# Convolution taps as ScalarE products, weight casts a unit ahead, and two more combined pairs of x in a one-core encoder block

## The chip, the cores and the metric

The kernel runs on one core of a Trainium2 chip. A core has TensorE (PE, matmuls into PSUM; PEld is its weight loads), VectorE (DVE), ScalarE (ACT), GpSimd (POOL) and SyncE (SP, which here only issues transfers). The metric is the device time in microseconds of one launch, lower is better; the time before is the median of 3 runs.

## The reference

One layer of a hybrid encoder on 256 tokens of width 4096, in float32:

```python
def reference(x, p, norm_in_g, w_in, rel_table, w_dw, b_dw, conv_ln_g, ..., final_g):
    ...
    xn = rms_norm(h, norm_in_g[i])
    proj = xn @ w_in[i]                     # 4096 x 14336
    q, k, v, z_a, a_c, g_c, z_c = jnp.split(proj, ..., axis=-1)
    y_a = chunked_attention(q, k, v, rel_table[i])   # 16 heads of 128, 4 chunks of 64
    y_a = rms_norm(y_a, attn_out_g[i]) * jax.nn.silu(z_a)
    y_c = conv_module(a_c, g_c, w_dw[i], b_dw[i], conv_ln_g[i], conv_ln_b[i], w_pw[i], b_pw[i])
    y_c = rms_norm(y_c, conv_out_g[i]) * jax.nn.silu(z_c)
    h = h + jnp.concatenate([y_a, y_c], axis=-1) @ w_out[i]
    gate = jax.nn.sigmoid(rms_norm(h, ple_norm_g[i]) @ w_ple_gate[i] + b_ple_gate[i])
    h = h + gate * (p[i] @ w_ple[i])
    return rms_norm(h, final_g)

def conv_module(a, g, w_dw, b_dw, ln_g, ln_b, w_pw, b_pw):
    u = a * jax.nn.sigmoid(g)
    ...     # causal depthwise convolution along time, 31 taps, + b_dw
    u = jax.nn.silu(layer_norm(u, ln_g, ln_b))
    return u @ w_pw + b_pw
```

## The kernel before

Activations lie transposed in SBUF: `xT` is eight `big` tiles of 4 blocks of 128 rows, each split into a high part (rounded to the matmul's float32r) and a low part. A product adds three matmuls for each 128 x 128 block of x and 512 columns of weights: high x high, low x high, high x low. So each weight tile `wt` (128 x 1024 floats, 512 KB by one transfer on SP's queue, five buffers) is split too: ScalarE casts it to `wh`, VectorE subtracts `wl = wt - wh` (lines 202 and 203 in `parts_of`, three buffers each).

There are two kinds of product. `product` takes 512 columns and runs over K in steps of two blocks (two row halves x two blocks x three = 12 matmuls a step, line 216). `mixed_product` takes two sets of 512 columns and runs over 16 *units* of two K blocks each. A plain unit has 24 matmuls (line 352). A unit marked `*` ("seven") is *combined*: by a 2 x 2 scheme with seven products instead of eight it needs 21 matmuls, and for it VectorE makes sums of weights (`ua`, `ub`, lines 399 to 404), which are split like weights; sums of x lie ready in `xS`. Its helper products P1, P5, P6, P7 take four banks of `ps_tmp`, the pool that the transposes and the attention use too; on the last combined unit `helper_sums` frees them. Which units are combined, and in which order, is a text such as `early = "1 3 5 7 0* 9 2* 11 4* 13 6* 15 8 10 12 14"`.

The order of the work: first `g_c` and `a_c` of 512 channels by `product`. Then four groups g. In each, `glu_conv(g + 1)` makes a and g of the next 512 channels by a mixed product with order `early`, gates and transposes them to `uT`, and queues their 31 x 4 taps in `later`: each one a VectorE instruction of 128 x 256 (line 594). `heads(g)` then makes q and k by another mixed product with `early`, transposes them, makes v by `product`, and runs the attention of four heads in one go. `fill(n)` after a unit takes n items from `later`: four in these mixed products, two in `product`. In the last group `layer_norm_swish` puts the layer norm in `later`, its sums on POOL. Then come the pointwise product (line 848), the gates z_a and z_c (`gated`, orders `delayed` and `dense`), the output product (`late`, `dense`), and the embedding gate (`late`, `steady`), the last two blocks of columns by `product`.

Apart from a few pinned instructions at the start, the order on each engine is laid out ahead of the run by a planner that takes the earliest instruction of the program that it expects to be ready. Each engine then runs its list in order.

Of the kernel before, what the change touches and what calls it, by code (L numbers as in the profile page):

```python
# [19 lines left out]
FIRST = 2  # L20
WARM = (5, 3, 2)
# [5 lines left out]
def hybrid_block(  # L27
# [31 lines left out]
    PAD = TAPS - 1  # L59
# [14 lines left out]
    wpool = pool("wpool", 5)  # L74
# [8 lines left out]
    upool = pool("upool", 2, first_sums)  # L83
    more = None

# [3 lines left out]
    pin = tc.keep_in_program_order  # L89


    gin_rows = spool.tile([KD, P], F32, tag="s", name="gin_rows")
# [3 lines left out]
    w_in0 = w_in[0]  # L96
# [11 lines left out]
    idle = spool.tile([P, NB], mybir.dt.bfloat16, tag="pT", name="idle")  # L108
# [84 lines left out]

    def part_tiles():
        return [wpool.tile([P, KC, NB], F32R, tag=tag, name=tag, bufs=3) for tag in ("wh", "wl")]

    def parts_of(wt, kc, tiles=None):
        if tiles is None:
            tiles = part_tiles()
        wh, wl = tiles  # L200
        made = (
            nc.scalar.copy(wh[:, :kc, :], wt[:, :kc, :]),  # L202
            nc.vector.tensor_tensor(  # L203
                wl[:, :kc, :], wt[:, :kc, :], wh[:, :kc, :].bitcast(F32), ALU.subtract
            ),
        )
        return (wh, wl), made
# [13 lines left out]

    def product(w, col, lhs, kblocks, pool=None, tag="acc", ahead=None, lag=(), begun=None, fills=2):
# [94 lines left out]
    def pair_parts(src):  # L317

        tiles = [upool.tile([P, 2, NB], F32R, tag=tag, name=tag) for tag in ("uh", "ul")]
        return parts_of(src, 2, tiles)[0]  # L320

    def units(text):

        return [(int(u.rstrip("*")), u.endswith("*")) for u in text.split()]


    steady = units("1 0* 3 2* 5 4* 7 6* 9 8* 11 10* 13 12* 15 14")
    dense = units("1 0* 3 2* 5 4* 6* 7 8* 9 10* 11 12* 14* 13 15")
    delayed = units("1 3 5 7 0* 9 2* 11 4* 13 6* 15 8* 10 12 14")
    early = units("1 3 5 7 0* 9 2* 11 4* 13 6* 15 8 10 12 14")  # L330
    late = units("1 3 5 7 9 11 13 15 0* 2 4* 6 8* 10* 12 14")

    def mixed_product(
# [29 lines left out]
        last_seven = max(n for n, (_, seven) in enumerate(order) if seven)  # L363
        for n, (pair, seven) in enumerate(order):
            if ahead:
                ahead(pair)
            wts = []
            for k in range(2):
                wt = wpool.tile([P, 2, NB], F32, tag="w", name="wt")
                kb = 2 * pair + k  # L370
                rows = w[kb * P : (kb + 1) * P, :]
                nc.sync.dma_start(
                    wt,
                    bass.AP(
                        tensor=rows.tensor, offset=rows.offset + col,
                        ap=[list(rows.ap[0]), [apart, 2], [1, NB]],
                    ),
                )
                wts.append(wt)
            if not seven:  # L380
                for k in range(2):
# [12 lines left out]
            w0, w1 = wts  # L394
            ua = upool.tile([P, 2, NB], F32, tag="u", name="ua")
# [665 lines left out]
```

## Time and profile before

| | us |
|---|---|
| median of 3 runs (2059.16 to 2062.18) | 2061.59 |
| span of the profiled execution (its time is given as this span) | 2059.9 |
| PE busy | 2031.9 (99%) |
| PEld busy | 1671.2 (81%) |
| DVE busy | 1823.0 (88%) |
| ACT busy | 1151.5 (56%) |
| POOL busy | 42.9 (2%) |

The profile is of one execution. "Busy" is the time in which an engine had an instruction running; recorded durations of neighbours overlap, so the spacing of starts is the better price. Ends of matmuls are modelled. Transfers moved 412.27 MB, 200 GB/s on average, with the 16 transfer engines' queue at 62.5%.

### The profile page before, as it was taken

The numbers are of one execution on the slowest core, as the hardware profiler recorded it, in microseconds if no ns is written. First come the engines' busy times: TensorE is split into PE (matmuls) and PEld (weight loads), VectorE is DVE, ScalarE is ACT, GpSimd is POOL, SyncE is SP. The second block draws the span as 40 slices with busy tenths as digits, with TensorE's granted clock in tenths as the row PEclk, the third lists the DMA queues.
The fourth block names the chain that finished last, engine by engine and source line by source line (L and its number), as shares of the span: only waits on it lengthen the run. The fifth ranks groups of instructions, "written<-read, shape, count | busy, mean of one in ns | idle before, by whom it ended". The sixth has DMA issues, their size and how long they took to land.

```text
span 2059.9 us, 25890 instructions
## 1 busy us (share of the span) xinstructions
PE 2031.9 (99%) x9145; PEld 1671.2 (81%) x9145; DVE 1823.0 (88%) x2543; ACT 1151.5 (56%) x1477; POOL 42.9 (2%) x37
## 2 busy tenths in 40 slices
PE   9999999999999999999999999999999999999997
PEld 6888888887888787788888888878888888888886
DVE  7599999999977998875889999899999999999954
ACT  7455535554564535575556656576565666656543
POOL 0000000000000002300000000000000000000010
PEclk9999999999999999999999999999999999999999
DMA  8666666656566665655666666676666656666664
GB/s 286 189 181 204 189 200 183 198 185 191 177 205 185 194 189 163 187 186 194 192 209 200 200 217 196 215 232 205 213 202 205 213 184 201 203 228 210 219 209 165
DMA packets 170331, 412.27 MB, mean 200 GB/s; under 512 B 13006, under 2 KB 16222, under 8 KB 170202
## 3 DMA queue, kind: packets, MB, share of 16 engines
q1 hardware_dynamic: 169914, 410.11, 62.5%
q8 instruction: 71, 1.16, 0.2%
q10 hardware_dynamic: 288, 0.52, 0.1%
q14 instruction: 58, 0.48, 0.1%
HBM read 406.39 MB, written 4.19 MB: 199 GB/s over the span
## 4 chain that ended last, share of the span: by engine, by line
PE 89%; DVE 6%; DMA 2%; issue 2%; ACT 1%; POOL 0%; SPq 0%; ACTq 0%; POOLq 0%; DVEq 0%
PE acc L352 53%; PE acc L216 21%; PE acc_P L352 13%; DVE wl L203 2%; DMA wt<-in_w_in_dram 1%; DVE cv L594 1%; DMA xin<-in_x_dram 1%; PE tmp_ps L161 1%; DVE ul L203 1%; PE tmp_ps L744 0%; PE tmp_ps L759 0%; PE tmp_ps L777 0%; ACT wh L202 0%; DVE ub L403 0%; PE tmp_ps L619 0%
## 5 line engine op out<-in xcount | busy, mean ns | idle before, releaser
L202 ACT CAST wh<-wt 128x1024 fp32r<-128x1024 f32 x739 | 726.0, 991 | 626.4 <-PE acc L352 314.0
L352 PE MATMUL acc<-wh,big_t 128*128 128x512 f32 x3344 | 1038.4, 391 | 3.6 <-ACT big_t L147 2.9
L203 DVE TENSOR_TENSOR wl<-wt,wh 128x1024 fp32r<-128x1024 f32 x739 | 849.7, 1161 | 130.0 <-ACT wh L202 124.4
L352 PEld LDWEIGHTS acc<-wh,big_t 128*128 128x128 f32 x3344 | 626.4, 188 | 133.1 <-ACT big_t L147 3.4
L352 PE MATMUL acc<-wl,big_t 128*128 128x512 f32 x1672 | 652.1, 391 | 3.4 <-DVE wl L203 3.3
L216 PE MATMUL acc<-wh,big_t 128*128 128x512 f32 x1248 | 389.2, 392 | 3.2 <-DVE big_t L148 1.3
L352 PEld LDWEIGHTS acc<-wl,big_t 128*128 128x128 f32 x1672 | 314.0, 188 | 72.0 <-DVE wl L203 7.3
L216 PEld LDWEIGHTS acc<-wh,big_t 128*128 128x128 f32 x1248 | 233.3, 188 | 52.7 <-DVE big_t L148 2.2
L216 PE MATMUL acc<-wl,big_t 128*128 128x512 f32 x624 | 243.1, 390 | 0.1
L594 DVE SCALAR_TENSOR_TENSOR cv<-uT,dw,cv 128x256 f32<-128x256 f32 x480 | 214.4, 487 | 1.0
L202 ACT CAST uh<-ub 128x1024 fp32r<-128x1024 f32 x103 | 108.4, 1052 | 113.2 <-DVE ub L404 92.1
L352 PE MATMUL acc_P<-uh,big_t 128*128 128x512 f32 x534 | 163.7, 390 | 0.0
L202 ACT CAST uh<-ua 128x1024 fp32r<-128x1024 f32 x103 | 108.5, 1054 | 62.4 <-DVE ua L400 57.9
L216 PEld LDWEIGHTS acc<-wl,big_t 128*128 128x128 f32 x624 | 117.1, 188 | 24.4 <-DVE wl L203 0.5
L203 DVE TENSOR_TENSOR ul<-ub,uh 128x1024 fp32r<-128x1024 f32 x103 | 128.2, 1245 | 8.1 <-ACT uh L202 7.6
L203 DVE TENSOR_TENSOR ul<-ua,uh 128x1024 fp32r<-128x1024 f32 x103 | 125.9, 1222 | 0.3
L352 PEld LDWEIGHTS acc_P<-uh,big_t 128*128 128x128 f32 x534 | 100.0, 188 | 21.2 <-ACT uh L202 0.5
L352 PE MATMUL acc_P<-ul,big_t 128*128 128x512 f32 x267 | 103.7, 393 | 0.9 <-DVE ul L203 0.8
L399 DVE TENSOR_TENSOR ua<-wt 128x512 f32<-128x512 f32 x103 | 71.6, 695 | 31.7 <-DMA wt<-in_w_in_dram 21.4
L400 DVE TENSOR_TENSOR ua<-wt 128x512 f32<-128x512 f32 x103 | 70.9, 689 | 3.7 <-DMA wt<-in_w_in_dram 3.0
L404 DVE TENSOR_TENSOR ub<-ub,wt 128x512 f32<-128x512 f32 x103 | 72.2, 701 | 1.2
L403 DVE TENSOR_TENSOR ub<-ua,wt 128x512 f32<-128x512 f32 x103 | 71.0, 689 | 0.2
(201 smaller groups left out, 1350.8 us busy)
## 6 DMA issues: line engine op xcount, KB each, us to landing
wt<-in_w_in_dram SPq DMA_DIRECT2D x447, 512.0 KB, 4.1
wt<-in_w_out_dram SPq DMA_DIRECT2D x128, 512.0 KB, 4.2
wt<-in_w_ple_gate_dram SPq DMA_DIRECT2D x128, 512.0 KB, 4.1
wt<-in_w_pw_dram SPq DMA_DIRECT2D x32, 512.0 KB, 4.4
hc<-in_x_dram SPq DMA_DIRECT2D x8, 512.0 KB, 5.0
wt<-in_w_ple_dram SPq DMA_DIRECT2D x8, 512.0 KB, 4.5
out_dram<-hc SPq DMA_DIRECT2D x16, 256.0 KB, 2.9
xin<-in_x_dram SPq DMA_DIRECT2D x7, 512.0 KB, 8.9
```

Of the source, the lines that this page charges most:

```text
L161: nc.tensor.transpose(pt[:, i * T + h * P : i * T + (h + 1) * P], src[:, h, b * P : (b + 1) * P], ident,)
L202: nc.scalar.copy(wh[:, :kc, :], wt[:, :kc, :]),
L203: nc.vector.tensor_tensor(wl[:, :kc, :], wt[:, :kc, :], wh[:, :kc, :].bitcast(F32), ALU.subtract),
L216: nc.tensor.matmul(acc, a, b[:, k, :], start=kb == 0 and kind == 0, stop=kb == kblocks - 1 and kind == 2,)
L352: nc.tensor.matmul(banks[name], a, b, start=name not in begun, stop=final and ends[name] == n and kind == 2,)
L399: plus(ua[:, 0], w0[:, 0], w0[:, 1])
L400: plus(ua[:, 1], w0[:, 1], w1[:, 1])
L403: plus(ub[:, 0], ua[:, 0], w1[:, 1])
L404: plus(ub[:, 1], ub[:, 0], w1[:, 0])
L594: nc.vector.scalar_tensor_tensor(cv[:, i, :], uT[:, i, k : k + T], dw[:, b, k : k + 1], cv[:, i, :], ALU.mult, ALU.add,)
```

## The change

- Each tap becomes four ScalarE activations (`tap_products`: u times the tap's column, into a tile `prod`) and one VectorE sum of 128 x 1024 (`tap_sum`), instead of four VectorE multiply-adds. The tile is shifted by the tap's offset, so `uT` needs no zeros in front.
- `plan` lists every unit in order; `prepare` issues the transfers and ScalarE casts of the next unit in the midst of the one before, and `take` hands them out. `chain` fixes the order of casts, subtractions, weight sums and taps on ScalarE and on VectorE as the program has it.
- `early` has six combined units instead of four, so `xS` has three tiles, made of six blocks of x.
- The ends of a group (scaling of the accumulators, gate, transposes, scores, values, squares) are put in `closing`, and each `fill` takes one step of it. Taps go by weight: one for a product, three for a sum; plain units of the groups' mixed products give four, combined ones none, steps of the value product four.
- Combined units add weights in place in `wt`; `wh` and `wl` have five buffers; first and last units of a product go bank by bank; PSUM copies of qT, kT and pT move to ScalarE, the layer norm's sums from POOL to VectorE.

```diff
+AG = (4,0)
+QK = (4,0)
+VF=4
+WB = 5
+HB = 5
...
-    upool = pool("upool", 2, first_sums)
+    upool = pool("upool", 3, first_sums)
     more = None
+    more_scratch = []
...
+    def chain(ins):
+
+        prev = last_of.get(ins.ins.engine)
+        if prev is not None:
+            tc.add_manual_dep(
+                ins.ins, prev.name,
+                mybir.DependencyInfo(mybir.DependencyClass.NoSync, mybir.DependencyReason.DATA),
+                reason="order of the parts",
+            )
+        last_of[ins.ins.engine] = ins.ins
+        return ins
...
+    closing = deque()
+
+    def step():
+        if closing:
+            closing.popleft()()
+
+    def finish_steps():
+        while closing:
+            step()
 
     def fill(n):
-        for _ in range(min(n, len(later))):
-            later.popleft()()
+        step()
+        credit[0] += n
+        while later and credit[0] > 0:
+            item = later.popleft()
+            weight, item = item if isinstance(item, tuple) else (1, item)
+            credit[0] -= weight
+            item()
+        if not later:
+            credit[0] = 0
...
     def part_tiles():
-        return [wpool.tile([P, KC, NB], F32R, tag=tag, name=tag, bufs=3) for tag in ("wh", "wl")]
+        return [wpool.tile([P, KC, NB], F32R, tag=tag, name=tag, bufs=HB) for tag in ("wh", "wl")]
 
     def parts_of(wt, kc, tiles=None):
         if tiles is None:
             tiles = part_tiles()
         wh, wl = tiles
         made = (
-            nc.scalar.copy(wh[:, :kc, :], wt[:, :kc, :]),
-            nc.vector.tensor_tensor(
+            chain(nc.scalar.copy(wh[:, :kc, :], wt[:, :kc, :])),
+            chain(nc.vector.tensor_tensor(
                 wl[:, :kc, :], wt[:, :kc, :], wh[:, :kc, :].bitcast(F32), ALU.subtract
-            ),
+            )),
         )
         return (wh, wl), made
...
+    early = units("1 3 5 0* 7 9 2* 11 4* 13 6* 15 8* 12 10* 14")
...
+    def prepare():
+
+        if prepared or not plan:
+            return
+        unit = plan.popleft()
+        w, col, apart, at, kind = unit
+        wts, highs = [], []
+        if kind == "one":
+            wt = wpool.tile([P, KC, NB], F32, tag="w", name="wt")
+            nc.sync.dma_start(
+                wt,
+                w[at * P : (at + KC) * P, col : col + NB].rearrange("(k q) n -> q k n", q=P),
+            )
+            wts.append(wt)
+        else:
+            for k in range(2):
+                wt = wpool.tile([P, 2, NB], F32, tag="w", name="wt")
+                kb = 2 * at + k
+                rows = w[kb * P : (kb + 1) * P, :]
+                nc.sync.dma_start(
+                    wt,
+                    bass.AP(
+                        tensor=rows.tensor, offset=rows.offset + col,
+                        ap=[list(rows.ap[0]), [apart, 2], [1, NB]],
+                    ),
+                )
+                wts.append(wt)
+        for k, wt in enumerate(wts):
+            n = 1 if kind == "seven" and k == 0 else 2
+            highs.append(part("wh"))
+            chain(nc.scalar.copy(highs[k][:, :n], wt[:, :n]))
+        prepared.append((unit, wts, highs))
+
+    def take(*unit):
+
+        prepare()
+        found, wts, highs = prepared.pop()
+        assert found[1:] == unit[1:] and found[0] is unit[0], (found, unit)
+        return wts, highs
...
-            wh, wl = weight_parts(w, col, k0, kc, lag[kept.index(k0)] if keep else None)
+            if lag:
+                wh, wl = weight_parts(w, col, k0, kc, lag[kept.index(k0)] if keep else None)
+            else:
+                (wt,), (wh,) = take(w, col, None, k0, "one")
+                wl = part("wl")
+                minus(wl, wt, wh)
+                prepare()
...
-    early = units("1 3 5 7 0* 9 2* 11 4* 13 6* 15 8 10 12 14")
...
-            wts = []
...
+            (w0, w1), (h0, h1) = take(w, col, apart, pair, "seven" if seven else "pair")
+            l0, l1 = part("wl"), part("wl")
             if not seven:
-                for k in range(2):
-                    wh, wl = parts_of(wts[k], 2)[0]
-                    for j in range(2):
-                        for h in range(NH):
-                            name = (("P2", "P3"), ("P4", "X"))[h][j]
-                            add(name, block(2 * pair + k, h), (wh[:, j], wl[:, j]), n, k == 1)
-                fill(fills)
+                for wt, wh, wl in ((w0, h0, l0), (w1, h1, l1)):
+                    minus(wl, wt, wh)
+                prepare()
+                fill(fills[0] if isinstance(fills, tuple) else fills)
+                parts = ((h0, l0), (h1, l1))
+                places = [(k, j, h) for k in range(2) for j in range(2) for h in range(NH)]
+                if n in (0, len(order) - 1):
+                    places = [(k, j, h) for j in range(2) for h in range(NH) for k in range(2)]
+                for k, j, h in places:
+                    name = (("P2", "P3"), ("P4", "X"))[h][j]
+                    add(name, block(2 * pair + k, h), [t[:, j] for t in parts[k]], n, k == 1)
                 continue
             begins = not helper
             if begins:
                 for name in ("P1", "P5", "P7", "P6"):
                     helper[name] = ps_tmp.tile([P, NB], F32, tag="tmp", name=f"acc_{name}")
                 banks.update(helper)
-            w0, w1 = wts
-            ua = upool.tile([P, 2, NB], F32, tag="u", name="ua")
-            ub = upool.tile([P, 2, NB], F32, tag="u", name="ub")
-            plus = partial(nc.vector.tensor_tensor, op=ALU.add)
-            w0h, w0l = parts_of(w0, 1)[0]
-            plus(ua[:, 0], w0[:, 0], w0[:, 1])
-            plus(ua[:, 1], w0[:, 1], w1[:, 1])
-            uah, ual = pair_parts(ua)
-            w1h, w1l = parts_of(w1, 2)[0]
-            plus(ub[:, 0], ua[:, 0], w1[:, 1])
-            plus(ub[:, 1], ub[:, 0], w1[:, 0])
-            ubh, ubl = pair_parts(ub)
+            minus(l0[:, :1], w0[:, :1], h0[:, :1])
+            plus(w0[:, 0], w0[:, 0], w0[:, 1])
+            minus(l1, w1, h1)
+            plus(w0[:, 1], w0[:, 1], w1[:, 1])
+            ah, bh = part("wh"), part("wh")
+            chain(nc.scalar.copy(ah, w0))
+            plus(w1[:, 1], w0[:, 0], w1[:, 1])
+            plus(w1[:, 0], w1[:, 1], w1[:, 0])
+            chain(nc.scalar.copy(bh, w1))
+            prepare()
+            fill(fills[1] if isinstance(fills, tuple) else fills)
+            al, bl = part("wl"), part("wl")
+            minus(al, w0, ah)
+            minus(bl, w1, bh)
...
+            add("P1", block(k0, 0), (h0[:, 0], l0[:, 0]), n, True)
+            add("P2", block(k1, 0), (h1[:, 0], l1[:, 0]), n, True)
+            add("P3", s_of(3), (h1[:, 1], l1[:, 1]), n, True)
+            add("P5", s_of(1), (ah[:, 0], al[:, 0]), n, True)
+            add("P7", s_of(0), (ah[:, 1], al[:, 1]), n, True)
+            add("P6", s_of(2), (bh[:, 1], bl[:, 1]), n, True)
+            add("P4", block(k1, 1), (bh[:, 0], bl[:, 0]), n, True)
...
-        for h, j in QUARTERS:
-            stt(
-                z[h][j], c[h][j], r[:, h : h + 1], z[h][j],
-                ALU.mult, ALU.subtract if j else ALU.add,
-            )
+
+        def finals():
+            for h, j in QUARTERS:
+                stt(
+                    z[h][j], c[h][j], r[:, h : h + 1], z[h][j],
+                    ALU.mult, ALU.subtract if j else ALU.add,
+                )
+
+        closing.append(finals)
...
+    def tap_products(made, uT, c, n):
+        dst = act.tile([P, 4, T], F32, tag="act", name="prod" if n else "cv")
+        made.append(dst)
+        for i in range(4):
+            b = 4 * c + i
+            chain(nc.scalar.activation(
+                dst[:, i, : T - n], uT[:, i, : T - n], AF.Identity,
+                scale=dw[:, b, TAPS - 1 - n : TAPS - n], bias=0.0 if n else bdw[:, b : b + 1],
+            ))
+
+    def tap_sum(made, n):
+        cv = made[0]
+        chain(nc.vector.tensor_tensor(cv[:, :, n:], cv[:, :, n:], made[n][:, :, : T - n], ALU.add))
...
+            sg, gate = scaled_pair(w_in0, o_a + c * NB, o_g - o_a, AG_ORDER, r_x, AG)
+
+            def gate_u():
+                for h in range(NH):
+                    nc.scalar.activation(gate[:, h, :], gate[:, h, :], AF.Sigmoid)
+                    tt(sg[:, h, :], sg[:, h, :], gate[:, h, :], ALU.mult)
+
+            closing.append(gate_u)
...
+        def begin_taps():
+            turn(1)
+            later.append((1, lambda: (tap_products(made, uT[0], c, 0), conv.append(made[0]))))
+            for n in range(1, TAPS):
+                later.append((1, lambda n=n: tap_products(made, uT[0], c, n)))
+                if n > 1:
+                    later.append((3, partial(tap_sum, made, n - 1)))
+            later.append((3, partial(tap_sum, made, TAPS - 1)))
+
+        closing.append(partial(turn, 0))
+        closing.append(begin_taps)
+        if c == 0:
+            finish_steps()
...
-        add = nc.gpsimd.tensor_tensor
+        add = nc.vector.tensor_tensor
...
+        closing.append(lambda: (turn(qT, q), load_bias()))
+        closing.append(lambda: turn(kT, k))
+        for hd in range(GH):
+            closing.append(partial(scores, hd))
+            if hd:
+                closing.append(partial(turn_p, hd - 1))
+        closing.append(partial(turn_p, GH - 1))
         if g == n_g - 1:
             first_sums.close()
             more = pool("more", 4)
-        accv = product(w_in0, o_v + g * NB, xT, KD)
-        v = spool.tile([P, NH, NB], F32, tag="hd", name="v", bufs=5)
-        for h in range(NH):
-            nc.scalar.activation(v[:, h, :], accv[h], AF.Identity, scale=r_x[:, h : h + 1])
-        attention(g, qT, kT, v, bias)
-
-    n_g = H // GH
+            second()
+        accv = product(w_in0, o_v + g * NB, xT, KD, fills=VF)
+        finish_steps()
+        closing.append(evacuate_v)
+        for hd in range(0, GH, 2):
+            closing.append(lambda hd=hd: (values(hd), values(hd + 1)))
+        closing.append(squares)
+
     assert n_g == CW // NB
-    xS = [big_tile(upool) for _ in range(2)]
-    for c in range(4):
+    xS = [big_tile(upool) for _ in range(3)]
+    for c in range(6):
...
```

More of the change, by code (lines that the diff above doesn't have):

```diff
@@ L106, in hybrid_block @@
         )
-    idle = spool.tile([P, NB], mybir.dt.bfloat16, tag="pT", name="idle")
+    idle = spool.tile([P, NB], mybir.dt.bfloat16, tag="s", name="idle", bufs=2)
     nc.vector.memset(idle, 0.0)
@@ L222, in product, with plus @@
+    def plus(out, a, b):
+        return chain(nc.vector.tensor_tensor(out, a, b, ALU.add))
     def product(w, col, lhs, kblocks, pool=None, tag="acc", ahead=None, lag=(), begun=None, fills=2):
@@ L1015, in hybrid_block @@
         if c < n_f - 1:
[L1016 removed]
+            acc = product(w_ple_gate0, c * NB, hT, KD)
             for h in range(NH):
```

277 lines of the change are left out of this document (145 added, 132 removed).

## The prediction

> **What bounds the kernel now.** I read the page first: busy shares, then the chain that ended last.
>
> ```profile
> span 2059.9 us, 25890 instructions
> PE 2031.9 (99%) x9145; PEld 1671.2 (81%) x9145; DVE 1823.0 (88%) x2543; ACT 1151.5 (56%) x1477; POOL 42.9 (2%) x37
> PE 89%; DVE 6%; DMA 2%; issue 2%; ACT 1%; POOL 0%; SPq 0%; ACTq 0%; POOLq 0%; DVEq 0%
> ```
>
> TensorE is busy 99% and holds 89% of the chain, VectorE 6%. Ends of matmuls are modelled, so the real rate is read from an unbroken run of the chain in order of time (start, length, what).
>
> ```profile
> 62.54 43.54 PE acc L216 x192
> 420.15 17.50 PE acc L352 x77
> ```
>
> 43.54/192 and 17.50/77 both give 0.227 us for one 512-column matmul. The kernel issues 8,619 such product matmuls (counted from the code): 8,619 x 0.227 = 1,955 us of the 2,059.9. What is left, some 105 us, is transposes and attention on TensorE, the start, the tail and waits. So two things can move the time: fewer matmuls, or fewer waits. The waits, by stage: TensorE and its weight loads between 107 us (convolution and attention groups begin) and 1,010 us (pointwise product ends), then the weight loads from 1,010 to 1,340 us.
>
> ```profile
> PE acc L352 <- DVE wl L203: 3.3, 4, 1.6
> PE tmp_ps L744 <- DVE z L462: 1.7, 2, 1.3
> PE acc_P L352 <- DVE ul L203: 0.8, 2, 0.5
> PEld acc L352 <- DVE wl L203: 7.3, 12, 2.0
> PEld tmp_ps L782 <- DVE pT L779: 3.1, 14, 0.6
> PEld tmp_ps L777 <- ACT s L770: 2.9, 10, 0.4
> PEld acc_P L352 <- DVE ul L203: 2.8, 6, 0.9
> PEld tmp_ps L744 <- DVE z L462: 2.7, 4, 1.8
> PEld acc L352 <- DVE z L874: 0.7, 1, 0.7
> ```
>
> Nearly all waits for VectorE are in the groups: 5.8 us seen on matmuls, 18.8 us on weight loads, of which part is covered by the matmul still running. I take 13 us of real loss, near the middle. The last row is the whole of 1,010 to 1,340 us: there is nothing to win in the gates, only something to lose. The stages:
>
> ```profile
> 0.00:38.00 38.00, 33.39 (x150) 23.86 (x151) 24.82 (x45) 27.65 (x61) 1.15 (x10) 1.00 0.89 312
> 38.00:107.40 69.40, 69.40 (x325) 57.50 (x325) 42.87 (x58) 35.97 (x47) 1.02 (x2) 1.00 0.64 192
> 323.70:548.00 224.30, 222.63 (x1013) 183.53 (x1012) 215.81 (x348) 114.52 (x143) 0.51 (x2) 1.00 0.62 190
> 1010.00:1340.00 330.00, 329.70 (x1456) 272.76 (x1455) 306.61 (x370) 195.63 (x217) 3.01 (x1) 1.00 0.64 205
> 1433.00:1680.00 247.00, 247.00 (x1096) 204.53 (x1095) 235.69 (x276) 147.68 (x175) 0.00 (x0) 1.00 0.62 206
> ```
>
> (stretch, length, then busy PE, PEld, DVE, ACT, POOL, granted clock, DMA share, GB/s). The clock is 1.00 throughout. One whole group, 323.7 to 548 us, has VectorE at 215.8 of 224.3 us and ScalarE at 114.5: VectorE is the engine that makes TensorE wait, ScalarE has room.
>
> **The change part by part.** Prices are spacings of neighbouring starts, since recorded durations overlap.
>
> ```profile
> 125.29 0.70 DVE L403 TENSOR_TENSOR ub<-ua,wt 128x512 f32<-128x512 f32 x1
> 125.89 0.49 DVE L594 SCALAR_TENSOR_TENSOR cv<-uT,dw,cv 128x256 f32<-128x256 f32 x1
> 126.29 0.70 DVE L404 TENSOR_TENSOR ub<-ub,wt 128x512 f32<-128x512 f32 x1
> 127.68 1.24 DVE L203 TENSOR_TENSOR wl<-wt,wh 128x1024 fp32r<-128x1024 f32 x1
> 128.82 1.24 DVE L203 TENSOR_TENSOR ul<-ub,uh 128x1024 fp32r<-128x1024 f32 x1
> ```
>
> So VectorE pays 0.60 for 512 columns, 0.40 for a tap, 1.14 for 1,024 columns.
>
> *Six combined pairs.* `early` goes from four to six combined units in 3 + 4 = 7 mixed products: 14 more combined units, each 21 matmuls instead of 24. 14 x 3 x 0.227 = **-9.5 us** of TensorE, which is on the path everywhere. Each costs VectorE 5 x 0.60 + 3 x 1.14 = 6.4 us against 2 x 1.14 = 2.3 for a plain one, so +8.2 us for two in a product. The third combined x tile adds two `combine_again`, about 5 us at these prices, to VectorE in 38 to 107 us, where 26 us are free (second stretch above): nothing.
>
> *Taps.* Per group VectorE loses 124 taps x 0.40 = 49.6 us and gets 30 wide sums x 1.14 = 34.2; the copies of qT, kT (4 x 0.60) and pT (4 x about 0.5) also go to ScalarE. Net for a group: 16.4 - 49.6 + 34.2 - 4.4 = -3.4 us, while TensorE's need falls 2.7. VectorE therefore stays near full; what changes is where its work lies. At before's four taps a unit a mixed product needed 12 x 2.3 + 4 x 6.4 + 64 x 0.40 + ends = 79 us plus some 5 for scalings and helper sums, against 84 us of matmuls. Afterwards it is 10 x 2.3 + 6 x 6.4 + about 8 x 1.14 + 5 = 76 against 83, and the value product takes 16 x 1.14 + 16 x 1.14 + 7 = 43 against 43.5 plus some 5 us of small TensorE work. That is cover, barely.
>
> ScalarE's price for a tap product (128x226 to 256, SBUF, one column as scale) is not in the trace. Its bounds:
>
> ```profile
> 890.59 1.63 ACT L712 CAST big_t<-cv 128x256 fp32r<-128x256 f32 x5
> 877.90 2.57 ACT L702 ACTIVATE cv<-cv,prm 128x256 f32<-128x256 f32 x5
> 1342.49 1.54 ACT L147 ACTIVATE big_t<-tmp_ps,prm 128x256 fp32r<-128x256 f32 x4
> 858.03 1.98 ACT L202 CAST wh<-wt 128x1024 fp32r<-128x1024 f32 x2
> ```
>
> Taking off a last instruction of 0.41, 0.59, 0.47 and 1.05 us, the spacings are 0.31 (no column operand), 0.50 (two), 0.36 (one, from PSUM) and 0.93. Nearest is one column: 0.39, between the ends. 496 x 0.39 = 193 us more ScalarE (ends 154 and 248), in all about 1,380 of 2,050. On average it lies beside TensorE; the tight place is a value product: 16 casts x 0.93 + 16 taps x 4 x 0.39 + exponentials, copies and table load about 9 = 49 us beside some 48.5. The casts run ahead there by up to four of the five `wh` tiles, so I cost it at nothing; at 0.50 it is 56 us, 7 too many, three times.
>
> The Trainium skill, "ScalarE: Activation LUTs", Rules for kernel authors, says the opposite of this edit: multiply and add belong on VectorE, not ScalarE. Its section What ACT_TABLE_LOAD costs gives 186 ns + 0.833 ns an element, 93 ns for each pointer operand, 93 ns of overlap back to back; my estimate from these figures at 241 columns is 0.387 us a tap, and the sum would be the same 2047. By the rule taken as a bound, the third rival below is the outcome; the 56% busy of ScalarE speaks against it.
>
> *Fixed order, casts a unit ahead.* No instruction is added; `chain` adds order, not waits. But a cast that waits for its weights now holds ScalarE's taps and PSUM copies behind it, and those hold TensorE's transposes. The combined unit also works in place in `wt`, so both weight tiles stay taken to the unit's end, with five as before; SP's queue already stands at that point:
>
> ```profile
> SPq L372 <- DVE wl L203: 939.8, 430, 6.7
> wt<-in_w_in_dram SPq DMA_DIRECT2D x447, 512.0 KB, 4.1
> ```
>
> The second tile of the next combined unit starts when the first tile of this one is freed: 4.1 us to land, 0.93 cast, 5.1 in all. VectorE covers it with its last subtraction 1.14, the plain unit 2.3 and the next unit's first two steps 1.2 = 4.6 plus a fill. So 0 to 0.5 us may be missing per combined unit. The gate and output stretches above leave VectorE 23.4 + 11.3 us idle over 29 + 24 combined units, 0.65 each: covered on average, not in every place. I take +2 us (ends 0 and 15).
>
> *Group ends spread out.* Scalings, transposes, scores and values come one step a unit, and first and last units fill and free banks one by one. This aims at the 13 us: L744, L777, L782 and the L203 waits where taps met the ends. Ends: 0 (they only move) and -13. I take -8, the larger part, since the arithmetic above gives VectorE 7 us of slack in a mixed product. The bias table is loaded later, two value units (5.4 us) ahead of its use, on SP's queue with its waits: I leave part of the 13 standing for it. The layer norm's sums move from POOL to VectorE, 6 x 1.14 + 2 x 0.9 = 9 us in the last group, where the convolution is over: no cost.
>
> *Start.* Each x chunk now stands behind one more 512 KB weight transfer on SP. At 312 GB/s that is 1.7 us; the stretch to 38 us has DMA at 0.89. Ends 0 and +1.7; I take +1.
>
> Sum: 2059.9 - 9.5 - 8 + 2 + 1 = 2045.4; the median of the runs is 1.7 above the profiled span, so **2047 us**. Not touched: gates, output and embedding products in count, and the tail.
>
> **Rivals.** *All waits go* and nothing new comes: 2061.6 - 9.5 - 13 = 2039. For it: all those waits name work the change moves. Against: VectorE still at 96% in the groups. *The waits only move*: 2061.6 - 9.5 + 3 = 2055, or with a few us more at each of 18 product boundaries no change, 2060. For it: VectorE's sum falls only as much as TensorE's. *ScalarE becomes the bound* of the value products at 0.50 us a tap: 3 x 7 to 3 x 10 us, 2047 + 25 = 2072; the point is about 0.45. *Slower by weight tiles*: in place, 75 combined units after 1,010 us each lose 1.0 us of VectorE against 0.65 of slack: 75 x 0.35 = 26, so 2045 + 26 = 2071; it decides from about 0.85 us each, and speaks through SP's 939.8 us of waits for exactly these tiles. Against: the 4.6 us of cover.
>
> **How the numbers follow.** Forecast (2040 to 2053) 0.45; all waits go (under 2040) 0.12; waits only move, 2053 to 2057.5, 0.13, and 2057.5 to 2065.7, 0.10; the two slower mechanisms 0.12 (tiles) and 0.08 (ScalarE). 0.2% of 2061.6 is 4.1 us, about what a measurement here tells from no change. So faster 0.70, same 0.10, slower 0.20. The range 2036 to 2066 leaves 0.04 below and 0.16 above.
>
> **What would show it.** 8,577 product matmuls at 0.227 us; no L594 group on VectorE, but some 496 ScalarE activations near 0.48 us recorded, 0.39 apart; ScalarE busy near 1,380 us, VectorE near 1,790. In one middle group 224.3 us should become about 217. Wrong if weight loads wait for ScalarE casts in the value products, if rows `PEld acc <- DVE wl` appear after 1,010 us with more than 5 us, or if the stretch 0 to 107 us grows by more than 2.

## The result and the profile after

The changed kernel takes 2046.76 us (median of 4 runs, 2045.93 to 2047.58) against 2061.89 for the one before (4 runs, 2059.16 to 2064.21): ratio 0.9928, 95% interval 0.9914 to 0.9942. 2047 was forecast. The profiled execution took 2046.57, 1.8 above its span. From the page: span, busy shares, the chain by engine, and the two groups that make the taps now.

```profile
span 2044.8 us, 26229 instructions
PE 2018.8 (99%) x9103; PEld 1667.0 (82%) x9103; DVE 1816.4 (89%) x2241; ACT 1370.8 (67%) x2033; POOL 14.7 (1%) x23
PE 95%; ACT 1%; DVE 1%; DMA 1%; issue 1%; ACTq 0%; POOLq 0%; POOL 0%; DVEq 0%
L714 ACT ACTIVATE prod<-uT,dw 128x255 f32<-128x255 f32 (+14 forms) x480 | 201.0, 490 | 3.7 <-DVE cv L721 3.6
L721 DVE TENSOR_TENSOR cv<-cv,prod 128x1020 f32<-128x1020 f32 (+14 forms) x120 | 138.5, 1154 | 20.3 <-ACT prod L714 20.2
```

VectorE's share of the chain fell from 6% to 1%, and TensorE's rose from 89% to 95%. With the 16 first taps, which carry the bias, there are 496 activations. The stretches that answer to those shown of before, with the same columns (start; a middle group; its value product; the pointwise product; the gates z; three output products):

```profile
0.00:104.70 104.70, 100.91 (x464) 79.99 (x465) 69.61 (x112) 65.53 (x110) 1.70 (x9) 1.00 0.74 239
323.10:542.30 219.20, 219.20 (x1002) 182.08 (x1001) 202.34 (x228) 179.17 (x304) 0.30 (x1) 1.00 0.62 197
492.70:542.30 49.60, 49.60 (x238) 41.23 (x237) 45.19 (x58) 49.46 (x104) 0.30 (x1) 1.00 0.61 185
901.20:995.50 94.30, 89.72 (x387) 73.31 (x386) 60.73 (x84) 49.28 (x74) 0.69 (x1) 0.96 0.61 201
995.50:1326.10 330.60, 330.40 (x1467) 273.59 (x1465) 314.13 (x374) 195.77 (x220) 1.67 (x1) 1.00 0.61 204
1416.90:1664.50 247.60, 246.97 (x1097) 204.09 (x1095) 241.83 (x281) 148.91 (x179) 0.00 (x0) 1.00 0.62 206
```

Two stretches of before that were not shown yet, its middle value product and its pointwise product:

```profile
503.30:548.20 44.90, 44.90 (x205) 37.23 (x204) 44.49 (x77) 16.78 (x17) 0.00 (x0) 1.00 0.62 188
916.80:1010.60 93.80, 93.80 (x434) 77.19 (x433) 60.08 (x91) 48.86 (x78) 0.69 (x1) 1.00 0.59 189
```

The middle group is full of TensorE work now (219.20 of 219.20) and 5.3 us shorter than before's 224.5 between the same two matmuls. In its value product ScalarE is busy for 49.46 of 49.60 us: full, but TensorE does not stand. The waits of TensorE from 107 to 1,010 us, and the first rows of those of its weight loads:

```profile
PE acc L255 <- ACT wh L304: 4.5, 1, 4.5
PE acc L446 <- DVE wl L321: 0.4, 1, 0.4
```

```profile
PEld acc L255 <- ACT wh L304: 5.0, 1, 5.0
PEld acc L446 <- DVE wl L321: 0.8, 1, 0.8
```

Before, the rows shown for VectorE came to 5.8 us on matmuls and 15.9 on weight loads here; with the row for ScalarE (2.9) the latter are the 18.8 of the prediction. Of VectorE's waits 0.4 and 1.9 us are left; in their place stands one wait of 4.5 to 5.0 us for ScalarE that had not been there. The timeline of its place, the start of the pointwise product (start, length, instruction):

```profile
899.51 5.00 ACT L852 CAST big_t<-cv 128x256 fp32r<-128x256 f32 x16
904.41 2.16 ACT L963 ACTIVATE y_a<-tmp_ps,den 128x128 f32<-128x128 f32 x8
906.42 0.66 ACT L562 ACTIVATE junk<-y_a 128x512 bf16<-128x512 f32 x1
...
907.65 4.85 ACT L304 CAST wh<-wt 128x1024 fp32r<-128x1024 f32 x5
908.77 1.22 PE L255 MATMUL acc<-wh,big_t 128*128 128x512 f32 x2 [4.54 <-ACT wh L304]
```

At the end of the last group the program issues what is left of the side work and of the group's end in one go. One weight unit was cast ahead; the second cast stands on ScalarE behind sixteen splits, eight evictions and the squares, until 907.65. The matmuls on both sides of the pause start at 903.84 and 908.77 us, 4.7 us further apart than usual. And the pause has an aftermath. The same place by the granted clock (third number from the right):

```profile
901.20:903.80 2.60, 2.60 (x14) 2.16 (x13) 2.60 (x9) 2.60 (x10) 0.00 (x0) 1.00 0.00 0
903.80:908.80 5.00, 0.46 (x3) 0.03 (x1) 1.97 (x8) 5.00 (x17) 0.54 (x1) 0.76 0.00 0
908.80:913.00 4.20, 4.16 (x9) 2.86 (x10) 4.20 (x4) 3.69 (x4) 0.15 (x1) 0.50 0.88 266
913.00:920.00 7.00, 7.00 (x31) 5.74 (x31) 3.96 (x4) 2.76 (x3) 0.00 (x0) 0.98 0.93 322
```

After the pause the clock is 0.50 for 4.2 us: matmuls start 0.427 us apart instead of 0.227. The Trainium skill, "TensorE: Matmul & The Clock Gate", What's actually happening, describes this: about 3.4 us of idleness halve the clock, and about as much work brings it back. The trace agrees on the half clock and, with some 4 us of work at it, roughly on the way back. It does not bear out the length of the pause: in run 4 below, pauses of 2.1 to 2.4 us are followed by a half clock too.

Where the 15.1 us of span went, with each stage counted from its first matmul to that of the next. "Beyond products" is what a stage takes over its product matmuls x 0.2267 us: small TensorE work and waits.

| | before | after | difference |
|---|---|---|---|
| product matmuls, 8,619 to 8,577 | | | -9.5 |
| start, to the first mixed product (105.92, 104.70) | | | -1.2 |
| four groups, beyond products | 46.5 | 41.6 | -4.9 |
| pointwise product, beyond products | 6.7 | 7.3 | +0.6 |
| all the rest | | | -0.1 |

Some small TensorE work moved from the pointwise product into the last group (434 matmuls in that stretch before, 387 after), so the two rows belong together: 53.2 us before, 48.9 after. Without the pause and its aftermath the pointwise product would take 1.65 us beyond its products (the first experiment), and the two together 43.2. The small matmuls are as many as before (9,145 - 8,619 and 9,103 - 8,577 are both 526), so the edits took 10.0 us of waits out of groups and pointwise product, and 5.6 came back there.

### The profile page after: what moved, and what is told of

It reads as the page before. It is cut to its first block, busy times and chain, and to the rows that moved or that the text cites. A ratio compares the mean times of both kernels' runs of the same rounds, so it can differ in the third digit from the quotient of the medians.

```text
span 2044.8 us, 26229 instructions
## 1 busy us (share of the span) xinstructions
PE 2018.8 (99%) x9103; PEld 1667.0 (82%) x9103; DVE 1816.4 (89%) x2241; ACT 1370.8 (67%) x2033; POOL 14.7 (1%) x23
## 4 chain that ended last, share of the span: by engine, by line
PE 95%; ACT 1%; DVE 1%; DMA 1%; issue 1%; ACTq 0%; POOLq 0%; POOL 0%; DVEq 0%
PE acc L446 56%; PE acc L255 22%; PE acc_P L446 15%; PE tmp_ps L179 1%; DMA wt<-in_w_in_dram 0%; DVE wl L321 0%; PE tmp_ps L886 0%; PE tmp_ps L922 0%; PE tmp_ps L944 0%; DMA wt<-in_w_out_dram 0%; ACT wh L304 0%; ACT big_t L852 0%; ACT junk L562 0%; DMA pin<-in_p_dram 0%; PE tmp_ps L134 0%
## 5 line engine op out<-in xcount | busy, mean ns | idle before, releaser
L321 DVE TENSOR_TENSOR wl<-wt,wh 128x1024 fp32r<-128x1024 f32 x961 | 1087.6, 1154 | 126.2 <-ACT wh L304 107.3
L304 ACT CAST wh<-wt 128x1024 fp32r<-128x1024 f32 x727 | 697.3, 981 | 298.9 <-PE acc L446 87.8
L324 DVE TENSOR_TENSOR wt<-wt 128x512 f32<-128x512 f32 x468 | 322.6, 689 | 11.3
L486 ACT CAST wh<-wt 128x1024 fp32r<-128x1024 f32 x117 | 123.3, 1054 | 211.1 <-DVE wt L324 189.2
L446 PE MATMUL acc_P<-wh,big_t 128*128 128x512 f32 x852 | 262.4, 390 | 1.0 <-ACT wh L489 1.0
L714 ACT ACTIVATE prod<-uT,dw 128x255 f32<-128x255 f32 (+14 forms) x480 | 201.0, 490 | 3.7 <-DVE cv L721 3.6
L446 PEld LDWEIGHTS acc_P<-wh,big_t 128*128 128x128 f32 x852 | 159.7, 188 | 34.5 <-ACT wh L489 1.5
L446 PE MATMUL acc_P<-wl,big_t 128*128 128x512 f32 x426 | 165.5, 390 | 0.0
L489 ACT CAST wh<-wt 128x1024 fp32r<-128x1024 f32 x117 | 123.3, 1054 | 56.1 <-DVE wt L324 41.2
L721 DVE TENSOR_TENSOR cv<-cv,prod 128x1020 f32<-128x1020 f32 (+14 forms) x120 | 138.5, 1154 | 20.3 <-ACT prod L714 20.2
L446 PEld LDWEIGHTS acc_P<-wl,big_t 128*128 128x128 f32 x426 | 79.9, 188 | 17.0 <-DVE wl L321 0.5
L166 DVE SCALAR_TENSOR_TENSOR big_t<-tmp_ps,prm,big_t 128x256 fp32r<-128x256 f32 x64 | 28.7, 476 | 2.2 <-ACT big_t L165 2.2
```

The costliest lines, as they stand in the source:

```text
L166: nc.vector.scalar_tensor_tensor(lo, src, scale, hi.bitcast(F32), ALU.mult, ALU.subtract),
L304: chain(nc.scalar.copy(highs[k][:, :n], wt[:, :n]))
L321: return chain(nc.vector.tensor_tensor(wl, wt, wh.bitcast(F32), ALU.subtract))
L324: return chain(nc.vector.tensor_tensor(out, a, b, ALU.add))
L446: nc.tensor.matmul(banks[name], a, b, start=name not in begun, stop=final and ends[name] == n and kind == 2,)
L486: chain(nc.scalar.copy(ah, w0))
```

## The experiments

Times are medians; "more" and "less" are against the 2046.76 of the changed kernel ("after") where no other run is named. The numbers in brackets are the ratio to the kernel before, measured beside the run, and its 95% interval. The kernel before measured 2061.5 to 2062.7 beside these runs, so differences of about 1 us between series are not read.

**1. The pause: the last splits inside the pointwise product.**

```diff
-    fill(1e9)
+    while len(later) > 12:
+        fill(1)
     finish_steps()
```

> The changed kernel, but the last twelve splits of the conv's outputs (ScalarE casts with their VectorE remainders) are no longer issued in one go before the pointwise product: they stay in its list of side work, two to each weight unit. Theory (ScalarE's pile-up of evacuations, squares and casts delays the second weight cast of the pointwise product): the 4.7 us pause of TensorE at 903.8 us and the half-speed matmuls after it go, the pointwise stage loses 4 to 6 us of its 7.3 us beyond its products, time about 2041 to 2043 us. Rival (the pause has another cause, the eviction of the conv's accumulators or the weight transfer): the stage keeps its 7 us, time 2046 to 2048 us. Second rival (the splits then come too late for the matmuls that read them): the wait moves into the pointwise product, 2046 to 2055 us.

Measured: 2042.58 us (ratio 0.9906, 0.989 to 0.9923), 4.2 less. The same two stretches:

```profile
903.80:908.80 5.00, 4.07 (x17) 2.69 (x17) 4.51 (x10) 5.00 (x12) 0.82 (x1) 1.00 0.66 225
908.80:913.00 4.20, 4.20 (x20) 3.50 (x19) 4.20 (x9) 4.20 (x8) 0.00 (x0) 1.00 0.72 231
```

A pause of 1.0 us is left, the clock stays at 1.00, and the stage falls from 94.33 to 88.70 us. The pile on ScalarE was the cause, and no wait moved to a later matmul of this product. The last of the gates z is 1.7 us longer in this run (85.45 against 83.71), so less comes through than the 5.6; why is not shown.

**2. Without the fixed order.** `chain` only returns its instruction; the planner places casts, subtractions, sums and taps.

```diff
     def chain(ins):
+        return ins
```

> The changed kernel without the fixed order: `chain` gives the instruction back and adds nothing, so the planner lays out casts, subtractions, sums and taps as it expects them to be ready. If the fixed order is what keeps VectorE's and ScalarE's parts ahead of TensorE, waits of 5 to 15 us come back in the groups: 2052 to 2062 us. Rival: the casts a unit ahead and the spread ends do it, and the order adds nothing: 2045 to 2049 us.

Measured: 2087.82 us (1.0128, 1.0111 to 1.0145), 41 more. Its waits of TensorE between 105 and 1,045 us:

```profile
PE acc_P L447 <- ACT wh L490: 12.0, 12, 1.3
PE acc L256 <- ACT wh L305: 4.9, 1, 4.9
PE acc_P L447 <- ACT wh L487: 4.5, 8, 0.9
```

`acc_P` are the helper products of combined units, `wh` L487 and L490 the casts of their sums: they come too late. (The second row is the pause of the pointwise product, which after has as well.) 40 of the 41 us lie in the seven gate and query/key products (the first one +13.3, then 1.7 to 8.3 each). It was expected to cost less; of the parts of the change that were taken away singly, it is the dearest.

**3. Without the lead of the casts.** The three calls of `prepare` inside the products go; `take` issues transfers and casts when the unit begins.

```diff
-                prepare()
...
-                prepare()
...
-            prepare()
```

> The changed kernel, but no weight unit is transferred and cast ahead: each unit's transfer and ScalarE casts are issued when the unit before it has had all its VectorE work and side work issued, instead of ahead of that side work and of its last subtractions; the fixed order of VectorE and ScalarE, the tap products, the six pairs stay. It splits the value of the fixed order (41 us with the cast ahead, by the run without any fixed order) into order and lead. If the lead carries it: casts arrive behind the tap products on ScalarE, waits at every unit of the gate, query/key and value stages, 2070 to 2100 us. If the order alone carries it: 2047 to 2055 us.

Measured: 2069.86 us (1.004, 1.0026 to 1.0053), 23 more, but not at every unit: the middle groups change by 0.3 us or less a product, except +0.9 in one value product. The first mixed product has +3.9, the last query/key product +13.5 and the last value product +6.5. The timeline of that query/key product:

```profile
807.33 1.99 ACT L304 CAST wh<-wt 128x1024 fp32r<-128x1024 f32 x2
...
810.87 1.12 DVE L718 TENSOR_TENSOR cv<-cv,prod 128x932 f32<-128x932 f32 x1
812.03 1.63 ACT L711 ACTIVATE prod<-uT,dw 128x232 f32<-128x232 f32 x4 [2.71 <-DVE cv L718]
813.56 1.56 ACT L304 CAST wh<-wt 128x512 fp32r<-128x512 f32 x2
814.20 0.69 DVE L321 TENSOR_TENSOR wl<-wt,wh 128x512 fp32r<-128x512 f32 x1 [2.21 <-ACT wh L304]
```

Here tap products wait for a wide sum (812.03, 2.71 us), and without a lead the next cast stands behind them and VectorE behind the cast. In the middle groups the taps do not wait for sums; that the five buffers of `wh` give the casts lead enough there was not tried with fewer. Both theories were half right: the lead is insurance, paid out where ScalarE is held up. That the tap products wait there because convolution and attention outputs share their pool of eight tiles is likely by the code, and was not tried.

**4. The taps on VectorE again**, four multiply-adds a tap in the fixed order, all else as after (shortened; the first tap of a group goes to VectorE too).

```diff
-    chain(nc.scalar.activation(dst[:, i, : T - n], uT[:, i, : T - n], AF.Identity, scale=..., bias=...))
...
-    chain(nc.vector.tensor_tensor(cv[:, :, n:], cv[:, :, n:], made[n][:, :, : T - n], ALU.add))
+    chain(nc.vector.scalar_tensor_tensor(cv[:, i, n:], uT[:, i, : T - n], dw[...], cv[:, i, n:], ALU.mult, ALU.add))
```

> The changed kernel with the taps as VectorE multiply-adds again, four of 128 columns by up to 256 for each, in place of four ScalarE products and one wide sum; the same weights in `fill`, the same order. ScalarE loses some 193 us, VectorE gains 30 x (1.6 - 1.14) = 14 us a group. By my sums a mixed product then needs about 80 us of VectorE against 83, a value product 50 against 48.5: 2 to 4 us a group come back, 2053 to 2060 us. Rival: with the ends spread VectorE has room enough and the tap edit is worth nothing, 2045 to 2049 us.

Measured: 2067.3 us (8 runs, 2063.82 to 2069.86; 1.0027, 1.0016 to 1.0037), 20.5 more. A gate product, which takes 85.67 us in after, and TensorE's longest waits in the groups:

```profile
328.60:416.70 88.10, 85.84 (x392) 71.21 (x390) 83.07 (x115) 49.86 (x64) 0.00 (x0) 1.00 0.60 193
```

```profile
PE acc L446 <- DVE z L552: 6.8, 3, 2.4
PE acc L255 <- DVE z L552: 4.3, 4, 1.4
```

L552 frees the accumulators at the end of a gate or query/key product: VectorE comes late to it. Part of the 20.5 us is clock: each of the three longest pauses in the groups, 2.1 to 2.4 us, is followed by some 3.4 us at half clock, first at 192.9 us.

```profile
192.90:196.20 3.30, 3.30 (x10) 2.53 (x9) 3.30 (x7) 1.10 (x2) 0.00 (x0) 0.50 0.40 138
```

Three times half of 3.4 us is an estimate of 5 us for it. The page's VectorE sum rises from 1816.4 to 1872.5 us, ScalarE's falls to 1180.6. The Trainium skill, "ScalarE: Activation LUTs", Rules for kernel authors, which the prediction weighed, puts multiply and add on VectorE; to follow it would cost 20 us here. The measurement decides: in this kernel VectorE is the engine that comes late.

**5. Dearer tap products.** The bias as a column of zeros, one operand more, for the 480 tap products without a bias (the expectation says 464; the page counts x480).

```diff
+    zero = cpool.tile([P, 1], F32, name="zero")
+    nc.vector.memset(zero, 0.0)
...
-    scale=..., bias=0.0 if n else bdw[:, b : b + 1],
+    scale=..., bias=zero if n else bdw[:, b : b + 1],
```

> The changed kernel, with the bias of the tap products given as a column of zeros instead of a number, so that every tap product of ScalarE reads one operand more: the same work, about 0.1 us dearer for each of the 464 products of a kernel that were 0.375 to 0.40 us apart. It puts the prediction's ScalarE rival (decides above about 0.45 us per product) to the test. Rival right: value products bound by ScalarE, 4 to 8 us more in each of the four value stages, 2060 to 2075 us. Cover (ScalarE idle time in the value products takes it): 2046 to 2050 us.

Measured: 2059.53 us (10 runs; 0.9986, 0.9977 to 0.9995), 12.8 more. The group of the products on its page, and the first group's value product:

```profile
L717 ACT ACTIVATE prod<-uT,zero,dw 128x255 f32<-128x255 f32 (+14 forms) x480 | 245.0, 583 | 2.6 <-DVE cv L724 2.3
```

```profile
274.00:326.30 52.30, 50.77 (x237) 40.69 (x236) 39.93 (x53) 52.27 (x103) 0.31 (x1) 1.00 0.52 154
```

The spacing of tap products goes from 0.390 to 0.482 us. 480 x 0.092 = 44 us of ScalarE, of which 12.8 come through: 1.3 to 3.2 us in each of three value products, 0.6 to 1.3 in the gate products and the last query/key product. Neither the cover nor the rival at its full price; the reserve of ScalarE in the value products is nearly used up at 0.39, where it is busy for 49.46 of 49.60 us.

**6. The weight sums in place, in the kernel before.**

```diff
-            plus(ua[:, 0], w0[:, 0], w0[:, 1])
...
+            plus(w0[:, 0], w0[:, 0], w0[:, 1])
...
```

> The kernel before, with the sums of weights made in place in the weight tiles instead of in tiles of their own, and nothing else. The prediction's rival says that a weight tile held until its sums are cast delays the next transfer: 0.85 us for each of the combined units would give 2071 us or more. If five tiles are enough: 2060 to 2064 us. It is also the base for the run with six pairs.

Measured: 2096.59 us (1.0169, 1.0154 to 1.0184), 34 more than before. Nearly all of it lies behind 1,012 us, 1.6 to 4.3 us in each of eleven products. The largest wait of its weight loads from 1,012 to 1,355 us, where before had 0.7 in all rows:

```profile
PEld acc_P L352 <- ACT uh L202: 11.1, 32, 1.1
```

So the casts of the sums come late. That held weight tiles make them late, as the rival has it, is not shown: the waits of VectorE and ScalarE for weight transfers, behind the pointwise product, rise from 21.5 us in before to 29.5, so by 8 of the 34. In place, a sum must also wait for the cast and the subtraction that read its tile; this was not tried apart.

**7. Six pairs in the kernel before**, on top of that, with the third tile of combined x that they need.

```diff
-    early = units("1 3 5 7 0* 9 2* 11 4* 13 6* 15 8 10 12 14")
+    early = units("1 3 5 0* 7 9 2* 11 4* 13 6* 15 8* 12 10* 14")
...
```

> The kernel before, with six combined pairs of x in the order of the gate and query/key products (14 combined units more, 42 matmuls fewer) and the sums of weights made in place, everything else as before. If the fewer products pay by themselves: about 9.5 us faster than before, 2052 us. If the old order of casts and sums cannot deliver the combined units in time (VectorE near its limit in these stages): no gain or a loss, 2060 to 2075 us.

Measured: 2133.24 us (1.0349, 1.0334 to 1.0365): 36.6 more than run 6, with 42 matmuls fewer. The first query/key product, and the weight loads' largest wait in the groups:

```profile
193.20:286.70 93.50, 87.90 (x377) 68.46 (x377) 92.74 (x142) 47.90 (x54) 0.00 (x0) 1.00 0.55 180
```

```profile
PEld acc_P L352 <- ACT uh L202: 26.0, 44, 2.0
```

VectorE is busy for 92.74 of 93.50 us. In the old kernel with sums in place the two pairs more are a loss; with the old sums in tiles of their own they were not tried. The changed kernel differs from this one in order, lead, taps and the buffers of `wh` and `wl` together; which of them makes the pairs pay is not separated.

**8. Four pairs in the changed kernel**, the reverse edit of `early`.

> The changed kernel with `early` back at four combined units; all else as changed. If the two added pairs are worth what their 42 matmuls cost TensorE, it takes 9.5 us more than the changed kernel: 2056 us, with as few waits in the groups. Rival: the added VectorE work of the combined units (8.2 us a product) ate part of it; then it takes less than 5 us more, 2048 to 2052.

Measured: 2051.9 us (0.9953, 0.9938 to 0.9968), 5.1 more. The gate and query/key products lose 13 us, 9.5 of them matmuls, but with two plain units more in each product the side work ends sooner, the pause at the pointwise product is not there (0.2 us of wait are left), and 7 us come back there and in the last value product. So 5.1 us is the price of the pairs less that of the pause; four pairs without the pile were not run.

**9. The group ends at once.** `finish_steps()` at each of the three ends.

```diff
+        finish_steps()
```

> The changed kernel with the ends of each group not spread: the steps in `closing` are all taken as soon as a product is done, as in the kernel before. If the spread ends removed the waits, 6 to 12 us come back in the groups, 2053 to 2059 us. Rival: the planner moves these steps among the next units by itself, as they are not in the fixed order: 2045 to 2049 us.

Measured: 2048.59 us (0.9938, 0.9924 to 0.9953), 1.8 more. Two middle value products lose 1.7 and 1.0 us, the last one 5.1, and the pointwise product wins 6.7, since its pile is then earlier. The two nearly cancel, so spreading the ends is worth next to nothing while the pile stands. Against run 1, which has no half clock there either, this run is 6.0 us slower; the two differ in both edits, so what spread ends are worth without the pile is open. That the planner moves the steps among the engines' work in any case, as the rival has it, was not looked at.

**10. Four weight tiles**, in the changed kernel.

```diff
-WB = 5
+WB = 4
```

> The changed kernel with four weight tiles in place of five, so that a weight tile that is held until its sums in place are cast bars the next transfer sooner. The prediction took +2 us for that holding with five tiles (0 to 15) and saw none. If the tiles were near their limit: waits of ScalarE's casts for transfers, mostly in the dense stages from 995 us on, 2055 to 2090 us. If there was plenty of room: 2046 to 2049 us.

Measured: 2185.17 us (1.0598, 1.058 to 1.0616), 138 more; of the 135.5 in the span 39 in groups and pointwise product, 91 after the first of the four gates z, 5.6 at the start. From the waits in the second gate z, with four tiles (1,124 to 1,214 us) and then with five (1,080 to 1,160 us):

```profile
ACT wh L304 <- DMA wt<-in_w_in_dram: 21.9, 15, 2.5
PEld acc_P L446 <- ACT wh L486: 5.1, 6, 1.4
```

```profile
ACT wh L304 <- DMA wt<-in_w_in_dram: 7.5, 6, 1.3
```

These are links of the chain that the weight-tile rival described: transfer late, cast late, sums late, helper products late. With five tiles its first link is there (7.5 us), and it ends before TensorE: the gate takes 81.60 us for 360 matmuls, with four tiles 91.27. Over the stages behind the pointwise product ScalarE's casts wait 215.2 us for weight transfers with four tiles and 52.5 with five.

**11. Seven pairs**, with edit 1 as the base.

```diff
-    early = units("1 3 5 0* 7 9 2* 11 4* 13 6* 15 8* 12 10* 14")
+    early = units("1 3 5 0* 7 2* 9 4* 11 6* 13 8* 15 10* 12* 14")
...
```

> The changed kernel with the last twelve splits inside the pointwise product and with seven combined pairs in the order of the gate and query/key products instead of six: seven combined units more, 21 matmuls fewer of 0.227 us, each unit 4.6 us more of VectorE. If VectorE's idle time takes them (it is busy for 76.7 of 85.7 us in the gate stage of the third group, 81 of 84 in the query/key stage, 45 of 49.6 in the value stage): 4.8 us less than the 2042.6 of six pairs, 2037 to 2040 us. If the query/key stage, which would need 85.5 us of VectorE, is now bound by it: 1 to 3 us of waits in each of four stages, 2042 to 2052 us.

Measured: 2069.67 us (1.0039, 1.0025 to 1.0053), 27 more than run 1. Neither theory: 19.5 of the 27 us lie in the last value product.

```profile
PE acc L255 <- ACT big_t L852: 10.1, 1, 10.1
PE tmp_ps L823 <- DVE sq L786: 5.8, 1, 5.8
```

TensorE waits for the layer norm. Plain units give side work four turns and combined units none, so seven products lose 28 turns, the convolution ends later, and its layer norm is done with nothing beside it. VectorE's own lack is the smaller part: three of the four query/key products, counted beyond their matmuls, are within 0.7 us of those with six pairs, the gate products 2.4 to 4.8 us above.

**12. Six weight tiles, with edit 1**: the version that beats both.

> The changed kernel with the last twelve splits inside the pointwise product and six weight tiles in place of five. Four tiles cost 138 us, so five may be near the edge too. If five still bar transfers: waits shrink in the places that are left (1.2 us at 1776 us, the second weight casts of some stages), 2038 to 2042 us. If five are enough, as the few waits left say (5.3 us of gaps over 0.3 us between 110 and 2040 us, most of them of other causes): 2042 to 2044 us, no difference to the 2042.6 of five.

Measured: 2039.67 us (2039.17 to 2039.72; 0.9894, 0.9878 to 0.9911).

```profile
span 2037.9 us, 26238 instructions
PE 2017.2 (99%) x9103; PEld 1666.8 (82%) x9103; DVE 1815.4 (89%) x2241; ACT 1366.5 (67%) x2033; POOL 14.8 (1%) x23
```

It is 2.9 us below run 1, though the intervals of the ratios overlap. 1.0 us of that is at the start; that x chunks and weights waited there for free tiles is not shown. The other 1.9 us are the last of the gates z (83.53 against 85.45 us), where run 1 has two waits of 0.7 and 0.6 us on TensorE and this run none.

## Why the prediction was right, point by point

The time was right, and so was the sign. Three of its terms were not (waits 3.6 us too hopeful, weight tiles 2 and the start 2.2 too dear), and they cancel to 0.6: that 2047 fits so closely is luck.

- *Products, -9.5*: right, 8,577 matmuls at 0.2267 us. What the pairs are worth depends on the rest: 5.1 in the changed kernel with its pile (run 8), a loss of 37 in the old one with sums in place (run 7).
- *Waits at group ends, -8 (0 to -13)*: mis-sized in both directions. 10.0 went, and 5.6 came back as the pause and half clock from 904 us on; net 4.4. The pile-up of the last group's leftovers on ScalarE was nowhere in it: of that place it asked only what the layer norm's sums cost VectorE. Its reason was also off: "group ends spread out" moves 1.8 us with the pile there (run 9), while order (41), lead (23) and taps (20.5) carry the result. These do not add up: each is the price of missing one part with the others there. And of the 18.8 us of weight-load waits that it put down to VectorE, 2.9 were for ScalarE.
- *Weight tiles, +2 (0 to 15)*: no loss showed. Its row, weight loads waiting for `wl` after 1,010 us, came out at 0.8, under the 5 that would have refuted the forecast. With one tile fewer the mechanism is there: 138 us. That the old kernel loses 34 us by sums in place (run 6), near the rival's 26, does not show it, since waits for transfers grow by 8 us there. What spares the changed kernel that loss is open: the four gates z take 330.6 us in after, 330.4 without the order (run 2), 332.3 without the lead (run 3) and 343.2 in run 6, so neither alone does it; the buffers of `wh` and `wl`, five instead of three, were not varied.
- *Start, +1*: wrong sign, -1.2. One weight transfer more in front of the x chunks did not cost there. The lead did not gain it, since without it the first mixed product begins at 104.64 us (run 3); which edit did was not tried.
- *ScalarE's price, 0.39*: 0.390 measured as the mean of 339 pairs of neighbours. The estimate from the figures of the Trainium skill, "ScalarE: Activation LUTs", What ACT_TABLE_LOAD costs, 0.387, agrees. ScalarE took 1370.8 us (1,380 predicted), a middle group 219.2 (217). VectorE took 1816.4; the 1,790 does not follow from the prediction's own terms, which give 1823.0 + 7 x 8.2 - 4 x 19.8 + 5 + 9 = 1,815.
- *ScalarE as the bound*: did not come true, but it was closer than its chance of 0.08 said. The point was put at 0.45, with a reserve of casts in front; ScalarE is full in the value products at 0.390 already, and 0.482 costs 12.8 us (run 5), less than the 21 to 30 of the rival at 0.50.

In a middle group what is left beyond the products, 9.7 us, is small TensorE work. So the rival "all waits go" describes the groups, and run 12, with two more edits, comes near its time of 2039.

## What to carry to other kernels

When an engine near its limit feeds the bound one, see to the order of the feeding work before adding to it: the planner's order costs 41 us in the changed kernel, and the same two pairs more lost 37 us in the old kernel and gained 5 in the changed one, of which the order is one part. Spread side work needs its end counted as well: whatever is left over is issued in one go, and a weight cast behind that pile stops the matmuls. For each ring of buffers, try one fewer and one more; here one weight tile fewer cost 138 us, and one more gained some 3.

## What the runs showed of the hardware that was not expected

A pause of 4.7 us cost TensorE nearly 7 us: for 4.2 us after it the granted clock was 0.50, matmuls started 0.427 us apart, and half of that time was lost too. A pause of 1.0 us at the same place (run 1) left the clock at 1.00. In between, length alone does not decide: pauses of 2.1 to 2.4 us in run 4 were followed by 3.4 us at 0.50, and one of 2.7 us in run 9 was not. And one column operand more makes an activation of some 241 columns 0.092 us dearer, at neighbours' spacing, as the Trainium skill's "ScalarE: Activation LUTs", What ACT_TABLE_LOAD costs, has it with 93 ns.
